# One adaLN step of the second layer amid the first layer's routing, ahead of the first experts' loads

## Chip, cores, metric

One core of one Trainium2 chip. The metric is device microseconds of one execution; of the profiled execution, the span and the granted clock of TensorE are shown beside it. TensorE (PE) multiplies, VectorE (DVE), ScalarE (ACT) and GpSimd (POOL) work on its operands and results, and SyncE (SP) issues nearly all loads and stores; GpSimd issues the indirect ones.

## What is computed

An attention block and then two layers on a main sequence of 512 tokens and a context of 256 tokens, 1024 wide, in float32. Each layer has a mixer (a convolution and a state space scan, with a layer norm and an RMS norm behind them and an output projection) and a mixture of experts: a gate over 4 groups of 4 experts, the two best experts of a token, each with a gate, an up and a down matrix. Both are modulated by adaLN vectors, which come from a condition vector `c` alone:

```
mod = silu(c) @ w_ada[l] + b_ada[l]      # 6 x 1024 per layer and sequence: shift, scale, gate; twice
h   = rmsnorm(x) * (1 + scale) + shift
x   = x + gate * f(h)                    # f: mixer, then experts
```

So layer 1's vectors depend on nothing that layer 0 computes, and may be worked out at any time before layer 1's modulation wants them.

## The kernel before

The kernel is written in Tile: the program gives the operations, a scheduler sets the order of each engine, and buffers come from pools in turn, so that a load waits until the last reader of its slot is done. Matrix products are done as three matmuls of a high and a low part: a weight comes by DMA as a tile of 512 KB (128 x 1024), ScalarE copies it into the high part (L260) and VectorE, or for some tiles GpSimd, subtracts that from it for the low part (L261). The pair is called a split below.

**adaLN.** `ada(l)` (L370) is a generator that makes layer l's vectors in three units u. A unit runs over k = 0 to 7; each k loads two tiles `raw` of `w_ada` (L256, through SP, pool `raw` with four slots) and does four matmuls (L387) into a PSUM tile `ad`. It yields after every second k, which is one step: four loads and eight matmuls. The last step of a unit also copies the sums (L392, ScalarE), turns them (L395) and adds the bias (L397, L405, VectorE). `fill(n)` (L410) advances the generators by n steps, `need(l, c)` until unit c is done. A layer has 12 steps. Where they are called is a table: `FILL[l]` and the strings `SF[l]`. Before, layer 1's steps 1 to 4 stand at the end of layer 0's mixer (`FILL[0][2]` = 4), 5 to 8 in layer 1's scan (`SF[1]` = '02209', L1020), and 9 to 12 behind that scan (the '9' at L885 runs the generator out), beside the convolution, its layer norm (mean L307 and L317, rstd L326 to L360, gelu and gain L897 to L903) and the norm of y (L910).

**Experts.** Layer 0 has six token tiles. At the end of the mixer the output projection (L276) writes `hT` and the context (loads `sg`, stores `cd`). The routing follows: logits (L1257, L1260), their norm (L326 to L335, L1264), bias (L1267), `tokens_out`, which turns the tokens (L1279), scales them (L1282 on VectorE, L1285 on ScalarE with L1286 on GpSimd) and writes them to `t_d` in DRAM (L1287), then the choice of group and experts (L1307 to L1326), lists of tokens (one-hots L1358, matmuls L1390, numbers L1366 to L1377) and the order of the later experts by load (L1598 to L1606, then L1612 and L1613 reorder the choices). An expert e then gathers its tokens (L1434, GpSimd), turns them (L1444), and does its hidden layer (L1474) and its output (L1516); results are scattered by GpSimd (L1535). The first three experts are fixed; later ones are taken by number from `eido` (L1606).

**Loads ahead.** The weights of the first experts are loaded before their turn. `AHEAD[0]` names them by place: a code c is expert c // 3 and its quarter c % 3 (0 and 1 gate and up, 2 down). At place 8 the string '2345' stands for e0's down, e1's two quarters and e1's down, eight loads. They take buffers as `RWS[0]` says, first four `raw`, then alternately `rawm` (four slots of the layer's own pool) and `raw`. `raw` is the pool that the adaLN loads use too.

**Places in the routing.** A small table of functions, `at`, is called at numbered places: position 0 right after the logits, then 1, 2 behind the choice of the experts, 3, 4 and 5 further on. `TPOS` says which function has which position; before, its third is 6, a position at which nothing is called, and `FILL[0][3]` is 0.

Of the kernel before, what the change touches and what calls it, by code (L numbers as in the profile page):

```python
# [34 lines left out]
XW = 1  # L35
HG = 2
HP = 0
FILL = ((1, 0, 4, 0), (0, 0, 0, 0))
SF = ('000111111', '02209')
SCP = (0, 0)  # L40
PB = (3, 3)
# [3 lines left out]
AHEAD = (('', '', '0', '1', '', '', '', '', '2345'), ('', '', '0', '1', '', '', '', '', '2345'))  # L45
TOKV = (0,)
RWS = ("wwwwwwww", "mmmmwwww")
TPOS = (0, 1, 6)

# [152 lines left out]
class Prog:  # L204
# [524 lines left out]
    def mixer(self, l):  # L729
# [4 lines left out]
        with E:  # L734
# [37 lines left out]
            full = [s for s in strs if s.full]  # L772
            self.fill(FILL[l][0])

# [138 lines left out]
            self.need(l, 12)  # L913
            self.fill(FILL[l][2])
            return full
# [149 lines left out]
    def moe(self, l, full):  # L1065
# [22 lines left out]
        with E:  # L1088
# [64 lines left out]
            def gate_up_half(e, q):  # L1153
                if isinstance(e, int) and (e, q) in early:
                    return early[e, q]
                return load_split(wgu_of(e, q), nc.gpsimd if q >= 2 - PL[l] else None)
# [19 lines left out]
            def down_half(e):  # L1176
                if isinstance(e, int) and (e, 2) in early:
                    return early[e, 2]
                return load_split(wd_of(e))

            def ahead(n):
                for c in AHEAD[l][n]:
                    e, q = divmod(int(c, 36), 3)
                    early[e, q] = down_half(e) if q == 2 else gate_up_half(e, q)
# [111 lines left out]
                    nc.scalar.activation(tt[:, 512 * hf:512 * hf + 512], pt, AF.Copy)  # L1296
                nc.sync.dma_start(dst, tt)

            at = dict(zip(TPOS, (tokens_out, lambda: ahead(8), lambda: self.fill(FILL[l][3]))))
            at.get(0, int)()  # L1300
            at.get(1, int)()
            self.mark(f"moe{l}-r")
# [550 lines left out]
```

## Time and profile before

| | |
|---|---|
| median of 3 runs | 1604.54 us (1602.48, 1604.54, 1607.76) |
| the profiled execution | 1599.32 us, span 1597.5 us |
| granted clock of TensorE, mean | 0.938 |
| TensorE busy | 1391.5 us (87%) |
| VectorE busy | 1014.9 us (64%) |
| ScalarE busy | 680.3 us (43%) |
| GpSimd busy | 230.9 us (14%) |
| moved by DMA | 260.79 MB, 163 GB/s in the mean |

Busy time counts instructions that work on data. The idle time before an instruction is given in brackets with what ended it, the releaser. Matmuls are pipelined, so a busy TensorE is not one at its peak. The layer 0 of the text lies between 300 and 1018 us of the span, its routing at 760 to 790; the end of layer 1's scan and norm lies at 1264 to 1305.

### The profile page before, as it was taken

The page shows a single profiled execution, that of the slowest core. Times are in us where ns is not written, and L with a number is a line of the kernel's source. Part 1 is how long each engine was busy: PE and PEld are TensorE (multiplying, and loading weights), DVE is VectorE, ACT ScalarE, POOL GpSimd, SP SyncE. Part 2 cuts the span into 40 slices and gives each one's busy share as a digit, 9 for nine tenths or more (in the row PEclk, how much of TensorE's full clock was granted, in tenths as well). Part 3 has the DMA queues.
Part 4 walks back from the last instruction along what each step waited for, and adds up shares of the span by engine and source line. Part 5 has one row for each costly group of instructions (what it writes and reads, how often), then busy time and mean ns, then how long its engine had stood idle before and what let it go on. Part 6 is the DMA issues. An engine that isn't in the chain of part 4 may idle for free. (4 is left out here: it accounts for less than half of the span.)

```text
span 1597.5 us, 20964 instructions
## 1 busy us (share of the span) xinstructions
PE 1391.5 (87%) x7422; PEld 975.8 (61%) x7422; DVE 1014.9 (64%) x2253; ACT 680.3 (43%) x1237; POOL 230.9 (14%) x205
## 2 busy tenths in 40 slices
PE   7899999979999998899578988589999989678964
PEld 6878766748888743467455566347885446454432
DVE  5877555548999765632783457368995464755445
ACT  5354455324542264433343456244433454424342
POOL 1111100000000221000442334000002200312113
PEclk9999999979999999899789999779999999799977
DMA  6111235221114067532559988602252763579974
GB/s 219 54 54 56 65 130 178 80 79 53 58 62 145 14 211 248 179 112 84 200 175 316 343 269 268 176 33 67 67 184 106 229 235 131 185 279 348 375 285 177
DMA packets 76476, 260.79 MB, mean 163 GB/s; under 512 B 9528, under 2 KB 11960, under 8 KB 76240
## 3 DMA queue, kind: packets, MB, share of 16 engines
q1 hardware_dynamic: 67872, 234.15, 41.8%
q0 software_dynamic: 8496, 25.28, 5.5%
q8 instruction: 59, 0.97, 0.2%
q14 instruction: 49, 0.40, 0.1%
HBM read 231.50 MB, written 33.55 MB: 166 GB/s over the span
## 5 line engine op out<-in xcount | busy, mean ns | idle before, releaser
L276 PE MATMUL mm<-act,uhi 128*128 128x512 f32 (+1 forms) x1504 | 323.3, 361 | 14.6 <-ACT uhi L260 7.7
L276 PEld LDWEIGHTS mm<-act,uhi 128*128 128x128 f32 x1504 | 248.3, 193 | 80.0 <-issue 13.3
L276 PE MATMUL mm<-act,ulo 128*128 128x512 f32 (+1 forms) x752 | 167.9, 357 | 0.6 <-DVE ulo L261 0.6
L276 PEld LDWEIGHTS mm<-act,ulo 128*128 128x128 f32 x752 | 124.9, 192 | 26.2 <-issue 5.1
L814 DVE SCALAR_TENSOR_TENSOR cvx<-vx,pr,cvx 128x456 f32<-128x456 f32 (+18 forms) x176 | 107.9, 616 | 2.3 <-ACT cvx L797 1.2
L260 ACT ACTIVATE uhi<-raw 128x1024 fp32r<-128x1024 f32 x58 | 61.2, 1058 | 109.2 <-PE mm L276 84.4
L387 PE MATMUL ad<-raw,sc 128*32 128x512 f32 x384 | 88.3, 649 | 12.5 <-DMA raw<-wada 12.0
L276 PE MATMUL mm<-whi,act 128*128 128x256 f32 x576 | 84.4, 292 | 10.2 <-ACT whi L260 10.0
L261 DVE TENSOR_TENSOR ulo<-raw,uhi 128x1024 fp32r<-128x1024 f32 x58 | 70.8, 1222 | 25.8 <-ACT uhi L260 9.2
L276 PEld LDWEIGHTS mm<-whi,act 128*128 128x128 f32 x576 | 76.1, 196 | 13.7 <-ACT whi L260 10.0
L1474 PE MATMUL mm<-part,uhi 128*128 128x512 f32 x168 | 55.0, 443 | 18.4 <-ACT part L260 11.8
L276 PE MATMUL mm<-act,whi 128*128 128x512 f32 x256 | 68.9, 411 | 0.2 <-ACT whi L260 0.2
L1474 PE MATMUL mm<-act,uhi 128*128 128x512 f32 x200 | 57.3, 405 | 0.2 <-ACT k L1524 0.2
L814 DVE SCALAR_TENSOR_TENSOR cvc<-vc,pr,cvc 128x241 f32<-128x241 f32 (+14 forms) x120 | 56.7, 472 | 0.5
L276 PEld LDWEIGHTS mm<-act,whi 128*128 128x128 f32 x256 | 47.2, 188 | 14.0 <-issue 3.5
L261 DVE TENSOR_TENSOR act<-rawm,act 128x1024 fp32r<-128x1024 f32 x30 | 39.9, 1331 | 24.3 <-ACT act L260 22.4
L1474 PEld LDWEIGHTS mm<-part,uhi 128*128 128x128 f32 x168 | 32.6, 209 | 32.1 <-ACT part L260 14.8
L1524 ACT ACTIVATE k<-mm 128x512 f32<-128x512 f32 x42 | 24.9, 595 | 60.4 <-PE mm L1516 41.2
L999 POOL TENSOR_TENSOR xw<-xstc,swgtc 128x512 f32<-128x512 f32 x8 | 9.7, 1232 | 278.3 <-ACT xstc L852 174.5
L1535 POOL DMA_INDIRECT acc<-k,idx x19 | 34.4, 1811 | 101.7 <-ACT k L1524 24.3
L261 DVE TENSOR_TENSOR wlo<-raw,whi 128x1024 fp32r<-128x1024 f32 x34 | 41.1, 1220 | 11.5 <-ACT whi L260 11.5
L261 DVE TENSOR_TENSOR act<-raw,act 128x1024 fp32r<-128x1024 f32 x32 | 38.9, 1222 | 14.7 <-ACT act L260 12.3
(528 smaller groups left out, 2828.4 us busy)
## 6 DMA issues: line engine op xcount, KB each, us to landing
raw<-wada SPq DMA_DIRECT2D x96, 512.0 KB, 5.0
raw<-wgu SPq DMA_DIRECT2D x42, 512.0 KB, 6.6
raw<-win SPq DMA_DIRECT2D x40, 512.0 KB, 3.5
rawm<-wgu SPq DMA_DIRECT2D x38, 512.0 KB, 6.8
raw<-wd SPq DMA_DIRECT2D x34, 512.0 KB, 6.4
act<-wgu SPq DMA_DIRECT2D x32, 512.0 KB, 8.5
rawm<-wd SPq DMA_DIRECT2D x30, 512.0 KB, 7.2
raw<-w SPq DMA_DIRECT2D x26, 512.0 KB, 4.6
```

The costliest lines, as they stand in the source:

```text
L260: self.nc.scalar.activation(hi, raw, AF.Copy)
L261: (eng or self.nc.vector).tensor_sub(lo, raw, hi.bitcast(F32))
L276: nc.tensor.matmul(out, lhsT=(ah, ah, al)[p], rhs=(bh, bl, bh)[p], start=(start and p == 0 and i == 0), stop=(stop and p == 2 and i == n - 1))
L387: nc.tensor.matmul(ps[32 * g:32 * g + 32], lhsT=self.sc[:, k, :], rhs=w[g // 2][:, 512 * (g % 2):512 * (g % 2) + 512], start=(k == 0), sto ...
L814: nc.vector.scalar_tensor_tensor(o_, v_, cw[:, l, i, k:k + 1], o_, op0=OP.mult, op1=OP.add)
L999: nc.gpsimd.tensor_tensor(hv(xw), hv(s.xst[:, c]), s.wgt[:, c, 8 * d:8 * d + 8, None].to_broadcast([128, 8, 64]), op=OP.mult)
L1474: nc.tensor.matmul(pg, lhsT=(xh, xl, xh)[p][:, 4 * q + k, :], rhs=(wh, wh, wl)[p][k // 2][:, 512 * (k % 2):512 * (k % 2) + 512], start=(n ...
L1524: nc.scalar.activation(y[:, o], py, AF.Copy)
L1535: nc.gpsimd.indirect_dma_start(out=acc[:, :], out_offset=bass.IndirectOffsetOnAxis(ap=j.sid[:, n:n + 1], axis=0), in_=y, in_offset=None, b ...
```

## The change

One step is put into layer 0's experts, between `tokens_out` and the loads ahead of place 8. Nothing is added: since the generator is taken one step further there, layer 1's scan gets steps 6 to 9 in place of 5 to 8, and three steps stand behind it in place of four. In layer 1 the same place calls `fill(0)`.

```diff
--- before.py
+++ after.py
@@ -35,7 +35,7 @@
 XW = 1
 HG = 2
 HP = 0
-FILL = ((1, 0, 4, 0), (0, 0, 0, 0))
+FILL = ((1, 0, 4, 1), (0, 0, 0, 0))
 SF = ('000111111', '02209')
 SCP = (0, 0)
 PB = (3, 3)
@@ -45,7 +45,7 @@
 AHEAD = (('', '', '0', '1', '', '', '', '', '2345'), ('', '', '0', '1', '', '', '', '', '2345'))
 TOKV = (0,)
 RWS = ("wwwwwwww", "mmmmwwww")
-TPOS = (0, 1, 6)
+TPOS = (0, 1)
 
 
 
@@ -1296,7 +1296,7 @@
                     nc.scalar.activation(tt[:, 512 * hf:512 * hf + 512], pt, AF.Copy)
                 nc.sync.dma_start(dst, tt)
 
-            at = dict(zip(TPOS, (tokens_out, lambda: ahead(8), lambda: self.fill(FILL[l][3]))))
+            at = {TPOS[0]: tokens_out, TPOS[1]: lambda: (self.fill(FILL[l][3]), ahead(8))}
             at.get(0, int)()
             at.get(1, int)()
             self.mark(f"moe{l}-r")
```

The order of instructions moves with it. On SP, at the end of layer 0's output projection, four slots of `raw` (the pool goes round) change hands; `wd` and `wgu` are down and gate/up weights, `wada` adaLN's. Before:

```order
L1137 DMA raw_6939<-wd 128x1024
L1237 DMA cd_6184<-sg_6477 128x256
L1234 DMA sg_6631<-cT 128x256
L1137 DMA raw_6945<-wd 128x1024
L1237 DMA cd_6184<-sg_6564 128x256
L1234 DMA sg_6706<-cT 128x256
L1137 DMA raw_6951<-wgu 128x1024
L1237 DMA cd_6184<-sg_6631 128x256
L1234 DMA sg_6773<-cT 128x256
L1137 DMA raw_6957<-wgu 128x1024
L1237 DMA cd_6184<-sg_6706 128x256
```

Now, from the third of the four adaLN loads on:

```order
L256 DMA raw_6948<-wada 128x1024
L1237 DMA cd_6184<-sg_6631 128x256
L1234 DMA sg_6773<-cT 128x256
L256 DMA raw_6950<-wada 128x1024
L1237 DMA cd_6184<-sg_6706 128x256
L1237 DMA cd_6184<-sg_6773 128x256
L1137 DMA raw_6956<-wd 128x1024
L1137 DMA raw_6962<-wd 128x1024
L1287 DMA t_d_6167<-k_1193_6849 128x1024
```

The four wada loads stand where e0's down and e1's first quarter stood; e0's down comes behind the context's last stores, and e1's six loads and four of e2's come behind the six writes t_d, of which the last row shows the first.

On TensorE, at the logits (L1260) and the token transposes (L1279), before:

```order
L1279 MATMUL mm_6886<-cs,rawm_6181 128x128
L1260 MATMUL ax_6819<-cs,t_1188_6820 128x33 x2
L1279 MATMUL ax_6850<-cs,k_1089_6174 128x128 x4
L1260 MATMUL ax_6819<-cs,t_1189_6824 128x33 x4
L1279 MATMUL ax_6865<-cs,k_1089_6174 128x128 x4
L1279 MATMUL ax_6880<-cs,rawm_6178 128x128 x2
```

Now:

```order
L387 MATMUL ad_6939<-raw_6940,sc 32x512
L1260 MATMUL ax_6819<-cs,t_1188_6820 128x33 x2
L1260 MATMUL ax_6819<-cs,t_1189_6824 128x33 x4
L1279 MATMUL ax_6850<-cs,k_1089_6174 128x128 x4
L1279 MATMUL ax_6865<-cs,k_1089_6174 128x128 x4
L387 MATMUL ad_6939<-raw_6940,sc 32x512
L387 MATMUL ad_6939<-raw_6942,sc 32x512 x2
L387 MATMUL ad_6939<-raw_6948,sc 32x512 x2
L387 MATMUL ad_6939<-raw_6950,sc 32x512 x2
L1279 MATMUL ax_6880<-cs,rawm_6178 128x128 x2
```

One L387 stands ahead of the logits, seven among the transposes.

On VectorE, at the start of the choice (L1307) behind the token writes (L1282), before:

```order
L1282 SCALAR_TENSOR_TENSOR k_1193_6849<-ax_6850,rt_6818,k_1092_6177 128x512
L1267 TENSOR_TENSOR mlg_6817<-mlg_6817,lb_6173 128x40
L1267 TENSOR_TENSOR mlg_6817<-mlg_6817,lb_6173 128x80
L1282 SCALAR_TENSOR_TENSOR k_1196_6864<-ax_6865,rt_6818,k_1092_6177 128x512
L1282 SCALAR_TENSOR_TENSOR k_1199_6879<-ax_6880,rt_6818,row_6183 128x512
L1282 SCALAR_TENSOR_TENSOR k_1202_6894<-ax_6895,rt_6818,row_6183 128x512
L1282 SCALAR_TENSOR_TENSOR k_1205_6909<-ax_6910,rt_6818,row_6183 128x512
L1307 TENSOR_REDUCE mgmx_6989<-mlg_6817 128x6
L1308 TENSOR_TENSOR mgoh_6990<-mlg_6817,mgmx_6989 128x24
L1409 TENSOR_TENSOR mge_6991<-mlg_6817,mgmx_6989 128x24
```

Now, with e0's down, whose splits stood in the output projection before (L261, `act<-raw`):

```order
L1282 SCALAR_TENSOR_TENSOR k_1196_6864<-ax_6865,rt_6818,k_1092_6177 128x512
L1282 SCALAR_TENSOR_TENSOR k_1199_6879<-ax_6880,rt_6818,row_6183 128x512
L1282 SCALAR_TENSOR_TENSOR k_1202_6894<-ax_6895,rt_6818,row_6183 128x512
L1282 SCALAR_TENSOR_TENSOR k_1205_6909<-ax_6910,rt_6818,row_6183 128x512
L261 TENSOR_TENSOR act_6959<-raw_6956,act_6958 128x1024
L261 TENSOR_TENSOR act_6965<-raw_6962,act_6964 128x1024
L1282 SCALAR_TENSOR_TENSOR k_1208_6924<-ax_6925,rt_6818,row_6183 128x512
L1307 TENSOR_REDUCE mgmx_7006<-mlg_6817 128x6
```

Two splits came in ahead of the last L1282 and L1307. Further on, on VectorE still, at the expert order (L1606) and the reordered choices (L1613), before:

```order
L1606 CAST eido_7131<-neidf_7127 128x13
L261 TENSOR_TENSOR ulo_7153<-ax_7161,uhi_7152 128x512
L1613 TENSOR_REDUCE mok_7168<-k_1313_7169 128x78
L1613 TENSOR_REDUCE mow_7177<-k_1315_7178 128x78
L261 TENSOR_TENSOR part_6978<-rawm_6975,part_6977 128x1024
L261 TENSOR_TENSOR part_6984<-raw_6981,part_6983 128x1024
L1423 CAST rc_6171<-mow_7177 128x6x13
L1377 CAST idx_1252_7031<-idf_7200 128x2
```

Now:

```order
L261 TENSOR_TENSOR ulo_7226<-ax_7227,uhi_7225 128x512
L261 TENSOR_TENSOR part_6995<-rawm_6992,part_6994 128x1024
L261 TENSOR_TENSOR part_7001<-raw_6998,part_7000 128x1024
L1606 CAST eido_7148<-neidf_7144 128x13
L1613 TENSOR_REDUCE mok_7185<-k_1318_7186 128x78
L1613 TENSOR_REDUCE mow_7194<-k_1320_7195 128x78
L1377 CAST idx_1257_7048<-idf_7217 128x2
```

The splits of e1's down (`part<-rawm`, `part<-raw`) changed places with L1606 and both L1613.

## Rows read from the trace of the kernel before

**Rows 1.** The page, part 1: busy time of the engines.

```profile
PE 1391.5 (87%) x7422; PEld 975.8 (61%) x7422; DVE 1014.9 (64%) x2253; ACT 680.3 (43%) x1237; POOL 230.9 (14%) x205
```

**Rows 2.** The page, a costly group (out<-in, count | busy, mean ns | idle before) and DMA issues.

```profile
L387 PE MATMUL ad<-raw,sc 128*32 128x512 f32 x384 | 88.3, 649 | 12.5 <-DMA raw<-wada 12.0
...
raw<-wd SPq DMA_DIRECT2D x34, 512.0 KB, 6.4
```

**Rows 3.** Busy us by stretch: PE, PEld, DVE, ACT, POOL; PEclk, DMA share, GB/s.

```profile
740.00:760.00 20.00, 20.00 (x102) 14.15 (x101) 7.19 (x8) 7.38 (x12) 0.00 (x0) 1.00 0.36 115
760.00:780.00 20.00, 8.86 (x64) 6.15 (x62) 14.25 (x43) 7.12 (x13) 7.45 (x6) 0.92 0.51 189
780.00:790.00 10.00, 2.96 (x46) 2.49 (x47) 9.10 (x29) 2.00 (x2) 4.50 (x3) 0.50 0.79 285
830.00:860.00 30.00, 28.84 (x156) 19.73 (x154) 15.42 (x48) 10.33 (x19) 11.87 (x8) 1.00 0.94 310
```

**Rows 4.** Timeline, TensorE, first experts: start, us, what, [idle before <-releaser].

```profile
789.23 1.97 PE L1444 MATMUL ax<-cs,k 128*128 128x128 f32 x8 [2.37 <-DMA k<-t_d,idx]
...
804.20 0.29 PE L1390 MATMUL op<-rc,oh 128*128 128x6 bf16 x6
...
808.00 1.94 PE L1444 MATMUL ax<-cs,k 128*128 128x128 f32 x8 [3.17 <-DMA k<-t_d,idx]
...
816.18 1.27 PE L1444 MATMUL ax<-cs,k 128*128 128x128 f32 x8 [2.29 <-DVE ulo L261]
819.33 1.22 PE L1516 MATMUL mm<-act,hl 128*128 128x512 f32 x2 [1.88 <-DVE hl L261]
...
823.46 1.62 PE L1474 MATMUL mm<-part,uhi 128*128 128x512 f32 x4
```

**Rows 5.** Timeline, SP's own queue, layer 1's adaLN loads.

```profile
1225.84 57.73 SPq L256 DMA_DIRECT2D raw<-wada  x28
```

**Rows 6.** Chain of waits, layer 1's conv and norm: start, us, what.

```profile
1267.86 4.55 DMA raw<-wada
...
1283.24 4.62 DMA raw<-wada
```

**Rows 7.** Timeline, TensorE, layer 0's routing.

```profile
767.80 0.63 PE L1279 MATMUL ax<-cs,rawm 128*128 128x128 f32 x4 [2.41 <-DVE mlg L1264]
```

**Rows 8.** Timeline, VectorE, layer 0's routing and first experts.

```profile
773.28 0.16 DVE L1307 TENSOR_REDUCE mgmx<-mlg 128x6 f32<-128x24 f32 x1
...
774.40 1.22 DVE L1309 TENSOR_TENSOR mgoh<-mgoh,cs 128x24 f32<-128x24 f32 x1
...
777.70 0.26 DVE L1309 TENSOR_TENSOR moh<-moh,cs 128x96 f32<-128x96 f32 x1
...
797.34 1.21 DVE L1613 TENSOR_REDUCE mow<-k 128x78 f32<-128x1014 f32 x1 [1.55 <-POOL k L1612]
798.46 1.22 DVE L261 TENSOR_TENSOR part<-rawm,part 128x1024 fp32r<-128x1024 f32 x1
```

**Rows 9.** Timeline, GpSimd, the same stretch.

```profile
770.59 4.99 POOL L1286 TENSOR_TENSOR k<-k,row 128x512 f32<-128x512 f32 x4
784.77 1.16 POOL L1434 DMA_INDIRECT k<-t_d,idx  x1 [9.19 <-DMA rawm<-wgu]
...
801.80 1.00 POOL L1434 DMA_INDIRECT k<-t_d,idx  x1 [4.50 <-DVE mow L1425]
807.26 1.20 POOL L1434 DMA_INDIRECT k<-t_d,idx  x1 [4.46 <-issue]
811.87 2.38 POOL L261 TENSOR_TENSOR act<-raw,act 128x1024 fp32r<-128x1024 f32 x1 [3.41 <-ACT act L260]
```

**Rows 10.** Timeline, SP's own queue, layer 0's token writes.

```profile
769.43 7.23 SPq L1287 DMA_DIRECT2D t_d<-k  x6
```

**Rows 11.** Timeline, ScalarE, layer 1's norm of y.

```profile
1290.02 0.62 ACT L304 ACTIVATE t2x<-yx 128x512 f32<-128x512 f32 x1
```

**Rows 12.** Timeline, VectorE, layer 1's norm of y.

```profile
1293.80 1.23 DVE L261 TENSOR_TENSOR ulo<-raw,uhi 128x1024 fp32r<-128x1024 f32 x1
```

## Prediction

> **What bounds the kernel now.** I read the page first: TensorE is the busiest engine, 1391.5 us, 87% of the span [rows 1], and the adaLN matmuls L387 cost it 88.3 us in 24 steps, 3.7 us a step, with 12.5 us of idle time before them, nearly all for the loads raw<-wada [rows 2]. Whether a moved step gains anything is decided by the two places that it leaves and enters, so I read those next, in the busy time by stretch and the timelines.
>
> The place it enters, layer 0's routing, is not bound by TensorE: from 760 to 780 us it works 8.86 us of 20, from 780 to 790 only 2.96 at a granted clock of 0.50 (the lower level, 1.2 GHz, after it had stood idle for most of ten us), while VectorE works 14.25 and 9.10 [rows 3]. It is a chain of small VectorE instructions that ends in the first gather. Ahead of it, 740 to 760, TensorE is full (20.00 of 20), and the chip's DMA engines work at 0.36 [rows 3]. Behind it come the first experts: TensorE stands 2.37, 3.17, 2.29 and 1.88 us for the first gather, the third, and two splits [rows 4], until the second half of the experts starts at 823.46; from 830 to 860 the DMA share is 0.94 and TensorE 28.84 of 30 [rows 3].
>
> The place it leaves is the end of layer 1's conv and norm. Of the 28 loads raw<-wada there, issued in 57.73 us, each takes 2.06 us [rows 5], and the chain of waits runs twice through them, 4.55 and 4.62 us [rows 6].
>
> **The change, part by part.** No step is added: 12 in layer 1's vectors before and after. One step is 4 loads of 512 KB, 8 matmuls (384 / 24 = 16 records) and no unit's end, so no L392, L395 or L397.
>
> *Layer 0, out-projection.* Four slots of `raw` that carried weights of e0's down and e1's first quarter now carry wada, so four splits leave ScalarE and VectorE. TensorE is full in that stretch [rows 3], so I take 0 here; at best 1 us.
>
> *Routing.* One L387 stands ahead of L1260: 3.7/8 = 0.5 us, 0.9 taken for that it delays both rows of logits. The other seven, 3.2 us, stand between the L1279 transposes. Before, TensorE idled 2.41 us there [rows 7]; so they push the later transposes by 0.9 + 3.2 - 2.4 = 1.7 us, and with them the token writes L1282. The two down splits of e0, 1.22 each (by the one at 798.46 [rows 8]), now stand on VectorE just ahead of the last L1282 and L1307 (third fence pair of the change). Their loads can issue only when the seven L387 have freed `raw`, near 769, and took 6.4 us to land at the page's median [rows 2], near 774 to 775; L1307 was at 773.28 [rows 8]. Then 2.4 us of splits follow: L1307 near 775 to 777, so +1.8 to +4. Against that, the first L1309, which took 1.22 us beside GpSimd's token adds where the next took 0.26 without them [rows 8], would come after the adds end at 775.58 [rows 9], which gives back 1.0. I take **+1.8** for the start of the experts, bounds 0.5 and 4.
>
> Here a rule is weighed. L1309 took 0.96 us longer beside GpSimd's adds, 1.25 us each, than alone [rows 8, 9]. The Trainium skill, SBUF — State Buffer, section "SBUF: two separate sides", says that a VectorE instruction with two SBUF inputs and a GpSimd instruction that reads SBUF share a port pair as a lock: whoever comes second stands still for the whole instruction. The rows agree. By it a split that falls among the adds would take 1.22 + 1.25 instead of 1.22, twice: +2.5 on the chain, a rival below; the sum leaves it out, since by the times above the splits fall at the adds' end.
>
> *SP and the loads.* e1's six loads now stand behind the six token writes t_d (first fence pair), so after 776.7 (769.43 + 7.23 [rows 10]); before, four of them and two of e2 were in SBUF by then. Ten loads go out there. The DMA share was 0.79 from 780 to 790 [rows 3], so the first gather, 784.77 to the tokens at 789.23 [rows 9, 4], shares with more: 0 to 1.7 us later (its later brother took 6.2, 801.80 to 808.00 [rows 9, 4]). I take 0 beyond the 1.8, for e1's weights are not wanted before 798.
>
> *Experts.* On VectorE the splits of e1's down now stand ahead of L1606 and both L1613 (last fence pair). Before, the second reduction ran from 797.34 to 798.55 and the splits came after it, from 798.46 on [rows 8]; now splits first, tied to ScalarE's split behind e0's first matmuls (+1.8), then 2 x 1.21: near 802.6. The third gather, 801.80 before, goes near 804.2, and its tokens stand at 810.4 (+2.4). e1's hidden layer has run by then in one piece. But the list L1390 for the next gather, at 804.20 before, now comes behind those tokens: 810.4 + 1.94 for the tokens and half a us of other work, 813; its gather, 3.1 us later as before (807.26), at 816; with 6.2 to land, tokens at 822.3 in place of 816.18; and L1516, which stands behind them, at 823.5 in place of 819.33 [rows 9, 4]. **+4.2** for the second half of the experts. Beyond 830 DMA and TensorE are both nearly full, so I let it pass to the layer's end whole. Bounds: +0.5 (TensorE's 3.17 + 2.29 + 1.88 = 7.3 us of idle time there swallow the rest) and +6.6 (a GpSimd split of 2.38 ahead of that gather, a rival).
>
> *Layer 1's tail.* Three steps instead of four. Four loads fewer are 8.2 us of queue, 3.7 us of TensorE. But between the two wada waits stands a chain that needs no wada: the layer norm's L326, L356, L360 and L902, then ScalarE's activations and splits in its order, up to L304 at 1290.02, for which the norm of y waits [rows 11]. It moves by the L387 taken out between L307 and L317, two pairs, 1.1 us. And VectorE now has both ulo splits, 1.22 us each, inside the y norm's rsqrt chain where one stood at 1293.80 [rows 12]: -1.1 + 1.2 = **0**; bounds -4 (half of the queue's 8.2) and +1.5.
>
> **Sum**: 0 + 4.2 + 0 = +4, on the profiled execution 1599.32 + 4 = 1603.3. That execution is 5.2 below the median of the runs shown, 1604.54; against it the forecast is 1608.5. A measurement of this kernel tells 0.3%, 4.8 us, from no change, so +4 counts as the same.
>
> **Rivals.**
> - *The tail comes free.* If the chain in layer 1 followed the loads, the queue's 8.2 us would go and the experts' 7.3 us of stalls layer 0's part: -8.2, 1596.3; with a part of it held by ScalarE, -6, 1598.5. For it: 4.55 and 4.62 us of the chain are wada [rows 6]. Against: ScalarE's queue at 1290.02. It decides if L304 of y starts over 3 us earlier.
> - *The fourth gather sticks behind GpSimd.* The split moved ahead of it (2.38 us [rows 9]) waits for ScalarE's half, whose load is now the tenth in SP's queue. From the point where that half is later than 816, the gather is at 818.4 or more, and the first gather pays its 1.7 too: 4.2 + 2.4 + 1.7 = +8.3, 1612.8. Slower.
> - *The port lock* on both down splits: 4.2 + 2.5 = +6.7, 1611.2. Slower.
> - *Hidden anyway.* The 1.8 us of the routing vanish in the experts' stalls and the tail gives nothing: 1604.5. For it: TensorE's 7.3 us of stalls between 808 and 823 [rows 4]. That the step would not move at all is excluded by the order of instructions.
>
> **How the numbers follow.** Forecast (+0.5 to +8, centre +4) 0.42, of which 0.28 within 0.3% and 0.14 above; tail free 0.24 (0.22 faster, 0.02 same); gather 0.17 and lock 0.05, slower; hidden 0.12, same. So faster 0.22, same 0.42, slower 0.36. The range goes from between these two prices of the free tail, 1597, to the gather's +8.3 with 2.2 for the routing's upper bound (4 for 1.8), 1615.
>
> **What would show it.** Right: four raw<-wada issued between 705 and 740; L1307 at 775 to 777; third gather near 804, tokens of the fourth near 822, e2's hidden 3 to 6 us later than 823.46 by the same origin; layer 1's y norm to out-projection unchanged within 1.5 us. Wrong: an L1307 no later than before, tokens of the fourth gather no later than 818, or a wait on raw<-wada gone from layer 1's chain with the out-projection 3 us or more earlier against the layer's start.

## Result and the profile after

| | before | changed |
|---|---|---|
| median | 1604.54 us (5 runs, 1600.15 to 1607.76) | 1618.46 us (5 runs, 1608.38 to 1619.34) |
| ratio to before | | 1.0105, 95% interval 1.0072 to 1.0138 |
| the profiled execution | 1599.32 us, span 1597.5 us | 1618.46 us, span 1616.7 us |
| granted clock, mean | 0.938 | 0.928 |

The change made the kernel slower by 1.05% by the ratio, some 17 us, and its median is above the 1615 that the range reached to. The two medians lie 13.9 us apart; all kernels below are compared by the ratio, whose intervals reach 0.2 to 0.3% to either side. The page of the changed kernel has TensorE 9 us busier for the same number of instructions, at a lower mean granted clock; VectorE and GpSimd are 2 us busier each, ScalarE is as before:

```profile
PE 1400.1 (87%) x7422; PEld 985.1 (61%) x7422; DVE 1017.2 (63%) x2253; ACT 680.8 (42%) x1237; POOL 233.1 (14%) x205
```

So no work was added; something waits. To see where, I count from the start of the first logits matmul L1260 (763.11 us before, 760.98 now, within what the kernels below, early5 apart, differ by at that point, 758 to 764). From there to layer 1's first residual (L1801) it takes 266.7 us before and 282.8 now, **+16.1**; from that to the last normalised y (L910) 272.9 and 276.6, **+3.7**; the rest of the span 294.8 and 296.3, +1.5. With the -2.1 of the start these make the 19.2 us between the two spans.

The busy time by stretch, as in [rows 3]: the stretch and its length, PE, PEld, DVE, ACT, POOL (instructions), granted clock, DMA share, GB/s.

```profile
740.00:760.00 20.00, 20.00 (x97) 12.87 (x95) 1.99 (x3) 4.39 (x10) 0.00 (x0) 1.00 0.04 14
760.00:780.00 20.00, 8.73 (x65) 5.74 (x64) 16.63 (x44) 7.96 (x12) 8.14 (x6) 0.87 0.63 231
780.00:790.00 10.00, 1.89 (x36) 1.48 (x36) 9.53 (x32) 3.17 (x3) 2.70 (x2) 0.50 1.02 392
830.00:860.00 30.00, 28.27 (x152) 22.19 (x151) 17.74 (x41) 13.62 (x23) 11.19 (x7) 0.95 0.66 194
```

From 740 to 760, where TensorE is full, the DMA share fell from 0.36 to 0.04: the adaLN loads were there by then, and SP's next loads wait for their slots. They go out at once later: 780 to 790 has 1.02 where 0.79 stood. And from 830 to 860 0.66 stands in place of 0.94.

TensorE's timeline behind the routing, as in [rows 4]:

```profile
790.55 1.97 PE L1444 MATMUL ax<-cs,k 128*128 128x128 f32 x8 [2.88 <-DMA k<-t_d,idx]
...
795.32 1.12 PE L1444 MATMUL ax<-cs,k 128*128 128x128 f32 x4 [1.60 <-DMA k<-t_d,idx]
...
814.15 1.94 PE L1444 MATMUL ax<-cs,k 128*128 128x128 f32 x8 [5.52 <-DMA k<-t_d,idx]
...
826.82 0.44 PE L1444 MATMUL ax<-cs,k 128*128 128x128 f32 x1 [7.53 <-DMA k<-t_d,idx]
826.92 1.20 PE L1516 MATMUL mm<-act,hl 128*128 128x512 f32 x2
...
832.44 1.37 PE L1474 MATMUL mm<-part,uhi 128*128 128x512 f32 x4
```

Counted from L1260, the first tokens stand at 29.6 us (26.1 before), the third at 53.2 (44.9), the fourth at 65.8 (53.1), after a wait of 7.53 us for their gather; e0's output (`hl`) right behind them at 65.9 (56.2), and e2's hidden layer at 71.5 (60.4). So the tokens' delay grows from gather to gather, +3.5, +8.3 and +12.7 us, and e2's hidden layer is 11.1 us late. VectorE's timeline, as in [rows 8], shows a large part of the reason:

```profile
770.87 4.33 DVE L261 TENSOR_TENSOR act<-raw,act 128x1024 fp32r<-128x1024 f32 x2
...
775.78 0.16 DVE L1307 TENSOR_REDUCE mgmx<-mlg 128x6 f32<-128x24 f32 x1
...
801.26 1.52 DVE L261 TENSOR_TENSOR part<-raw,part 128x1024 fp32r<-128x1024 f32 x1
802.69 0.47 DVE L1606 CAST eido<-neidf 128x13 int32<-128x13 f32 x1
...
804.19 1.19 DVE L1613 TENSOR_REDUCE mow<-k 128x78 f32<-128x1014 f32 x1
...
817.03 1.22 DVE L261 TENSOR_TENSOR act<-rawm,act 128x1024 fp32r<-128x1024 f32 x1
818.16 2.33 DVE L1377 CAST idx<-idf 128x2 int32<-128x2 f32 x1
```

The two splits of e0's down in the routing took 4.33 us in place of 2.44; e1's down splits end at 802.78, and only then come L1606 and both L1613, to 805.38 (798.55 before). A split stands ahead of the fourth list's numbers (817.03), and their conversion L1377 took 2.33 us, where the one of the third list, at 805.31, took 0.15. GpSimd, as in [rows 9]:

```profile
768.17 3.74 POOL L1286 TENSOR_TENSOR k<-k,row 128x512 f32<-128x512 f32 x3
772.17 1.95 POOL L1286 TENSOR_TENSOR k<-k,row 128x512 f32<-128x512 f32 x1 [0.26 <-ACT k L1285]
...
785.01 1.16 POOL L1434 DMA_INDIRECT k<-t_d,idx  x1 [10.89 <-DMA raw<-wgu]
...
806.22 1.00 POOL L1434 DMA_INDIRECT k<-t_d,idx  x1 [2.63 <-DVE ulo L261]
818.02 2.44 POOL L261 TENSOR_TENSOR act<-raw,act 128x1024 fp32r<-128x1024 f32 x1 [10.81 <-ACT act L260]
820.76 0.96 POOL L1434 DMA_INDIRECT k<-t_d,idx  x1 [0.30 <-DVE wsl L1396]
```

GpSimd's adds ran beside the first pair of slow VectorE instructions (768.17 on), its split at 818.02 beside the slow L1377, and the fourth gather stands behind that split, at 820.76, 59.8 us from L1260 (44.1 before). SP's queue shows what is late behind it. The loads of a pair of later experts (`act<-wgu`, L1145, eight issues) go out in all kernels here some five us after e2's hidden layer has begun; the first of them, before:

```profile
829.52 13.70 SPq L1145 DMA_DIRECT2D act<-wgu  x8
```

and in the changed kernel, where the row above it is one of the experts' own loads ahead, now behind the token writes:

```profile
776.34 1.22 SPq L1137 DMA_DIRECT2D raw<-wgu  x2
...
837.27 15.42 SPq L1145 DMA_DIRECT2D act<-wgu  x8
```

The pair's loads are 7.75 us later, 9.9 counted from L1260, and take 1.7 us longer to issue.

### The profile page after: what moved, and what is told of

Its sections match the earlier page's. It is cut to its first block, busy times and chain, and to the rows that moved or that the text cites. A ratio compares the mean times of both kernels' runs of the same rounds, so it can differ in the third digit from the quotient of the medians.

```text
span 1616.7 us, 20964 instructions
## 1 busy us (share of the span) xinstructions
PE 1400.1 (87%) x7422; PEld 985.1 (61%) x7422; DVE 1017.2 (63%) x2253; ACT 680.8 (42%) x1237; POOL 233.1 (14%) x205
## 5 line engine op out<-in xcount | busy, mean ns | idle before, releaser
L260 ACT ACTIVATE uhi<-raw 128x1024 fp32r<-128x1024 f32 x58 | 61.1, 1058 | 108.7 <-PE mm L276 81.3
L387 PE MATMUL ad<-raw,sc 128*32 128x512 f32 x384 | 89.6, 661 | 5.0 <-DMA raw<-wada 4.5
L261 DVE TENSOR_TENSOR ulo<-raw,uhi 128x1024 fp32r<-128x1024 f32 x58 | 70.8, 1222 | 25.7 <-ACT uhi L260 9.4
L1474 PE MATMUL mm<-part,uhi 128*128 128x512 f32 x168 | 56.3, 451 | 20.0 <-ACT part L260 12.8
L261 DVE TENSOR_TENSOR act<-rawm,act 128x1024 fp32r<-128x1024 f32 x30 | 42.1, 1404 | 26.6 <-ACT act L260 24.5
L1474 PE MATMUL mm<-act,uhi 128*128 128x512 f32 x200 | 56.4, 403 | 1.4 <-ACT k L1524 1.4
L1444 PE MATMUL ax<-cs,k 128*128 128x128 f32 x232 | 35.6, 301 | 20.6 <-DMA k<-t_d,idx 20.6
L1474 PEld LDWEIGHTS mm<-part,uhi 128*128 128x128 f32 x168 | 33.5, 214 | 32.8 <-ACT part L260 14.2
L261 DVE TENSOR_TENSOR part<-rawm,part 128x1024 fp32r<-128x1024 f32 x26 | 31.6, 1223 | 29.4 <-ACT part L260 21.2
L1235 DVE SCALAR_TENSOR_TENSOR hT<-mm,mod,hT 128x512 f32<-128x512 f32 x16 | 12.0, 751 | 60.0 <-PE mm L276 60.0
```

What stands on the lines that cost most here:

```text
L260: self.nc.scalar.activation(hi, raw, AF.Copy)
L261: (eng or self.nc.vector).tensor_sub(lo, raw, hi.bitcast(F32))
L387: nc.tensor.matmul(ps[32 * g:32 * g + 32], lhsT=self.sc[:, k, :], rhs=w[g // 2][:, 512 * (g % 2):512 * (g % 2) + 512], start=(k == 0), sto ...
L1444: nc.tensor.transpose(pt[:, 128 * k:128 * k + 128], j.xg[:, 512 * hf + 128 * k:512 * hf + 128 * k + 128], self.ident)
L1474: nc.tensor.matmul(pg, lhsT=(xh, xl, xh)[p][:, 4 * q + k, :], rhs=(wh, wh, wl)[p][k // 2][:, 512 * (k % 2):512 * (k % 2) + 512], start=(n ...
```

## The experiments

The theory after this reading (A): what costs is that e0's and e1's loads changed places with the step's, and that the splits, which go where their loads are, stand ahead of the lists that the third and fourth gather need; layer 1 gives nothing back. The rivals: the routing costs over 20 and layer 1 gives some back (B); the step's own work costs wherever it stands in the routing (C), or its matmuls delay the routing (E).

**early5.** The step elsewhere, ahead of the output projection.

```diff
-FILL = ((1, 0, 4, 1), (0, 0, 0, 0))
+FILL = ((1, 0, 5, 0), (0, 0, 0, 0))
```

> The moved step stands at the end of layer 0's mixer with the four others (five there), the routing is left alone, layer 1's tail has one step fewer as in the change. Theory A (the first experts of layer 0 lose because loads and splits changed places; layer 1's tail gives nothing): the step's 3.7 us of TensorE ahead of the projection and no gain in layer 1, 0 to +4 us against the kernel before, layer 0's tokens of the fourth list no later than before relative to the logits. Theory B (layer 1's tail gives back 4 to 8 us and the routing costs over 20): -4 to 0 us, and layer 1 from its start to the end of the norm of y is 4 us or more shorter than before.

Measured: 1.0019 of before (0.9995 to 1.0043), +3 us. The logits start 5.2 us later than before (768.28), the fourth tokens at 53.4 from there (53.1 before). Layer 1 from its first residual to the last y took 276.1 us (272.9): no relief. Theory B falls.

**behind.** The step at the same place of the program, behind the loads.

```diff
-            at = {TPOS[0]: tokens_out, TPOS[1]: lambda: (self.fill(FILL[l][3]), ahead(8))}
+            at = {TPOS[0]: tokens_out, TPOS[1]: lambda: (ahead(8), self.fill(FILL[l][3]))}
```

> The same step at the same place in the program, but behind the loads ahead of place 8 in place of ahead of them, so e0's down and e1's first half quarters keep their slots and their early issue. Theory A (displaced loads and the splits behind them): most of the loss goes, 0 to +6 us against before in place of +14. Theory C (the step's own loads and matmuls in the routing, wherever in it): still +10 to +14.

Measured: 0.9972 (0.9944 to 1.0000), 4.5 us faster than before, with an interval that reaches to no change. e2's hidden layer starts 55.3 us from L1260. The same loads and matmuls in the same routing cost nothing once the experts' loads go first: C falls.

**dummy.** A copy of the step in the routing, layer 1 untouched.

```diff
-            at = {TPOS[0]: tokens_out, TPOS[1]: lambda: (self.fill(FILL[l][3]), ahead(8))}
+            def dummy():
+                ps = self.psum("ad", 1)
+                for k in range(2):
+                    w = [self.load(I["wada"][1, 0, k][:, 1024 * i:1024 * i + 1024]) for i in range(2)]
+                    for g in range(4):
+                        o = 512 * (g % 2)
+                        nc.tensor.matmul(ps[32 * g:32 * g + 32, :512], lhsT=self.sc[:, k, :],
+                                         rhs=w[g // 2][:, o:o + 512], start=(k == 0), stop=(k == 1))
+            at = {TPOS[0]: tokens_out, TPOS[1]: lambda: (l == 0 and dummy(), ahead(8))}
```

> The kernel before with an extra copy of one step (four loads, eight matmuls, its sums used by nothing) at the place of the change; layer 1 keeps all its steps, as before. It prices the routing alone. Theory A: layer 0 as in the change, +14 us, and layer 1 as before, so +12 to +17 in all, the same as the change. Theory B: +18 to +25, since the relief of layer 1 is missing.

Measured: 1.0088 (1.0059 to 1.0117), +14 us, the change's loss within the intervals; e2's hidden at 70.9. Layer 0 from L1260 to layer 1's first residual took 281.4 us (282.8 in the change). So the loss is layer 0's, as theory A expected, and the step taken out of layer 1 is worth nothing that shows.

**after_pl and before_pl.** GpSimd's share of the splits in layer 0 given to VectorE, in the changed kernel and in the kernel before.

```diff
-PL = (1, 0)
+PL = (0, 0)
```

> The changed kernel with GpSimd's share of the splits of layer 0's second quarters given to VectorE. Theory A1 (the fourth gather stands behind GpSimd's split and its numbers wait for that split on VectorE): the wait of 7.53 us ahead of the fourth tokens falls to 3 or less and the kernel gains 3 to 6 us on the change. Theory A2 (the late list, behind the third tokens, is what counts): the wait falls by 2 to 3 us only and the time stays within 3 us of the change, or is worse by VectorE's extra work.

> The kernel before with GpSimd's splits of layer 0 given to VectorE, the control for the same edit to the change, which brought that back to the time before. If the edit repairs what the change spoils (the fourth gather behind GpSimd's split), this one is within 4 us of the kernel before. If GpSimd's splits are a loss in the later experts of either kernel, this one is 8 us or more faster.

Measured: the changed kernel so edited 1.0006 (0.9980 to 1.0032), 16 us less than the change; the kernel before 0.9944 (0.9920 to 0.9968), 9 us faster. So the first looked like a repair, and the control shows that half of it is a gain of its own: against before_pl the change still costs 1.0006 / 0.9944 = 1.0062, 10 us. The fourth tokens' wait of 7.53 us is gone (0.63, for TensorE's own work), but they stand at 63.3 from L1260, since the third are later, at 57.7. A1 was right on the wait; its gain of 3 to 6 us was too small. The control came out as the second reading of its expectation had it, 8 us or more faster. Of that gain one place is found: between 820 and 1000 us TensorE's largest wait for a GpSimd split (L1474 for `part`, 4.3 us, once) is gone in before_pl. The rest of the 9 us isn't accounted for.

**after_pl2.** One split alone, e2's second quarter, from GpSimd to VectorE.

```diff
-                return load_split(wgu_of(e, q), nc.gpsimd if q >= 2 - PL[l] else None)
+                return load_split(wgu_of(e, q), nc.gpsimd if q >= 2 - PL[l] and not (isinstance(e, int) and e == 2) else None)
```

> The changed kernel with one split alone, that of e2's second quarter, given from GpSimd to VectorE: the one that the change put ahead of the fourth gather. If that split is what makes the loss, the wait of 7.53 us ahead of the fourth tokens falls to 4 or less and the kernel is 4 to 8 us faster than the change, +6 to +10 against before. If the late list behind the third tokens makes it, the wait stays over 5 and the kernel within 3 us of the change.

Measured: 1.0049 (1.0031 to 1.0067), 9 us less than the change, for one instruction. On TensorE the fourth tokens still wait, 5.27 us, now for VectorE's split `act<-raw`, which took the place of GpSimd's:

```profile
820.17 2.07 PE L1516 MATMUL mm<-act,hh 128*128 128x512 f32 x4 [0.39 <-ACT hh L260]
...
827.68 1.94 PE L1444 MATMUL ax<-cs,k 128*128 128x128 f32 x8 [5.27 <-DVE act L261]
```

The order is that of the change: four matmuls of e0's output (`hh`, from 820.17), the fourth tokens, then the rest. So the wait came as the second reading had it and the time as the first (+8 us against before, of +6 to +10). The fourth gather goes out at 58.3 us from L1260, only 1.5 earlier than in the change, and e2's hidden layer 2.4 earlier (69.1 and 71.5). From L1260 to layer 1's first residual it is 276.8 and 282.8, so 3.6 us more are won behind e2's start; the later stages of the two profiled executions differ by 1 us. That this one split counts for much of the loss is shown; how it does, beyond the 2.4, is not.

**after_a234 and before_a234.** e1's down taken out of the loads ahead, in the changed kernel and before; it is then loaded in e1's turn. On VectorE L1606 and both L1613 stand ahead of its splits again.

```diff
-AHEAD = (('', '', '0', '1', '', '', '', '', '2345'), ('', '', '0', '1', '', '', '', '', '2345'))
+AHEAD = (('', '', '0', '1', '', '', '', '', '234'), ('', '', '0', '1', '', '', '', '', '2345'))
```

> The changed kernel with e1's down taken out of the loads ahead of place 8, so that it is asked for in e1's turn; on VectorE L1606 and both L1613 stand ahead of its two splits again, as before the change, while e0's down splits stay in the routing and the step stays where it is. Theory A (the late expert order and reordered choices, and with them the third and fourth gather): most of the loss goes, 0 to +6 us against the kernel before, and the fourth tokens stand 8 us or more earlier than in the change relative to the logits. Theory A0 (the routing's own delay and the adaLN step's loads): still +11 or more.

> The same edit to the kernel before, a control: by every theory within 4 us of the kernel before. If it is 6 us or more faster, the edit helps by itself and says less about the change.

Measured: 1.0040 (1.0021 to 1.0060), +6.4 us, and 0.9983 (0.9961 to 1.0005) for the control. The third tokens are at 49.4 us from L1260 (53.2 in the change), the fourth at 60.5 (65.8): 5.3 earlier, not 8. The fourth gather stands ahead of GpSimd's split again. This repairs 10 us of 17, and 1.0040 / 0.9983 = 1.0057 is left.

**after_both.** Both edits to the changed kernel (the `AHEAD` line of after_a234 and the `load_split` line of after_pl2).

> The changed kernel with both repairs at once: e1's down asked for in its turn, and e2's second quarter split by VectorE. If the two repair one thing (the third and fourth gather being late), the time is as with either, +5 to +8 us against before. If they repair two things that add, it is back at the time before, -2 to +2.

Measured: 1.0030 (1.0007 to 1.0052), +4.8 us; e2's hidden at 66.8. Together they repair little more than after_a234 alone (1.0040), which is nearer to one thing mended (+5 to +8) than to two (-2 to +2), though the interval, +1.1 to +8.3 us, touches both. With either edit the fourth gather no longer stands behind GpSimd's split, but it is 5.3 us earlier than in the change in after_a234 and 1.5 in after_pl2, so this need not be what they have in common. What makes the 0.3% that is left no run tells.

**dummyload.** The dummy step with matmuls of 32 columns: the loads without TensorE's 3.7 us, layer 1 untouched.

```diff
-                        nc.tensor.matmul(ps[32 * g:32 * g + 32, :512], lhsT=self.sc[:, k, :],
-                                         rhs=w[g // 2][:, o:o + 512], start=(k == 0), stop=(k == 1))
+                        nc.tensor.matmul(ps[32 * g:32 * g + 32, :32], lhsT=self.sc[:, k, :],
+                                         rhs=w[g // 2][:, o:o + 32], start=(k == 0), stop=(k == 1))
```

> The kernel before with four extra adaLN loads at the place of the change and matmuls of 32 columns only, which free the slots; layer 1 as before. GpSimd's split stands behind the fourth gather here, as before the change. Theory A: what is left without the late fourth gather is e0's down splits in the routing and e1's loads behind the token writes, +5 to +8 us. Theory E (the step's matmuls in the routing delay it): 0 to +2.

Measured: 1.0012 (0.9985 to 1.0039), +2 us. The time is theory E's (0 to +2), its mechanism is not: the routing ends as late as in the change (L1329 19.6 us from L1260; 17.5 before, 19.9 in the change). The fourth tokens are as late too (64.9), but on TensorE all of e0's output (`hl` from 61.1) stands ahead of them, where in the change `hl` stands behind; GpSimd's split is behind the fourth gather, which goes out at 53.4 (59.8 in the change); and e2's hidden layer starts at 65.7. So late tokens by themselves cost little here: a wait counts by what is queued behind it. And the loads' displacement by itself, which is the same in this kernel as in dummy, does not make the loss either. Which of the two, the order on TensorE or the one on GpSimd, makes the difference to dummy's 14 us this run doesn't tell.

**warm2.** Theory D, from layer 1's windows below: 12 matmuls, whose sums nobody uses, added to layer 1's tail of the kernel behind.

```diff
                     self.put_split(s.mx, i, v)
+                    if l == 1:
+                        px = self.mm()
+                        for g in range(3):
+                            nc.tensor.matmul(px[32 * g:32 * g + 32], lhsT=self.sc[:, i, :],
+                                             rhs=s.mx[0][i].bitcast(F32), start=True, stop=True)
```

> The kernel with the step behind the loads (0.28% faster than before), with 12 added matmuls in layer 1's tail whose sums nobody uses, fed by the layer norm's results, so that TensorE has work where the taken step left it idle. Theory D (in the tail TensorE falls to the lower clock for want of work, and that eats the relief): the granted clock between 255 and 270 us after layer 1's first residual goes from 0.50 to near 1.00, the sums L307 and L347 for the norm of y from 1.9 to 1.1 us, and the norm of y ends 1 to 3 us earlier than in that kernel, the median 1 to 3 us below it. If ScalarE's order alone holds the tail, the clock rises and the time stays within 1 us or gets worse.

Measured: 0.9975 (0.9955 to 0.9994) of before, where the kernel behind has 0.9972: no difference that can be told, so the time is as the rival reading had it. Inside the profile the clock rose as said, L307 and L347 took 1.05 us each (1.75 and 1.86 in behind), and the stage took 271.5 us to the last y where behind took 273.6. The stretches, columns as above:

```profile
1277.50:1282.50 5.00, 4.79 (x32) 1.40 (x32) 2.95 (x6) 4.38 (x9) 0.00 (x0) 1.00 0.63 221
1282.50:1287.50 5.00, 4.84 (x27) 4.06 (x25) 3.47 (x11) 2.08 (x3) 0.00 (x0) 1.00 0.23 66
```

against the kernel behind at the same distance from layer 1's first residual (255 to 260 and 260 to 265 us):

```profile
1278.70:1283.70 5.00, 1.91 (x10) 1.11 (x10) 2.61 (x6) 4.62 (x9) 0.00 (x0) 0.94 0.68 259
1283.70:1288.70 5.00, 4.31 (x14) 3.12 (x13) 1.75 (x8) 2.49 (x3) 0.00 (x0) 0.50 0.00 0
```

That the added matmuls brought the clock back is shown. The 2.1 us of the stage agree with it in one execution each, but lie within what the kernels differ by there (272 to 277), and the end of the program does not show them.

**behind_pl_a234.** The three edits whose ratio was below 1 by themselves, together; of the three, only before_pl's interval lies clear of 1.

> The step behind the loads, GpSimd's splits of layer 0 given to VectorE, e1's down asked for in its turn: each was faster than before by itself (0.28%, 0.56%, 0.17%). If they add: 1.0% faster than before, 1585 us by a median of 1600. If they gain from the same waits: 0.5 to 0.6%.

Measured: 0.9946 (0.9929 to 0.9963), 7.1 us faster in the median (1594.31). So they do not add; that they gain from the same waits is the reading of the expectation, and no run shows which. It and before_pl (0.9944) are the fastest kernels of the study, faster than both that were compared.

What goes with the order of the kernels is the start of e2's hidden layer (its first L1474, on `part`), counted from the first L1260, both from TensorE's timeline, in us:

| kernel | e2's hidden | first `act<-wgu` | ratio |
|---|---|---|---|
| behind | 55.3 | 61.0 | 0.9972 |
| before_a234 | 55.5 | 60.9 | 0.9983 |
| warm2 | 55.5 | 61.1 | 0.9975 |
| before | 60.4 | 66.4 | 1 |
| early5 | 60.7 | 66.8 | 1.0019 |
| dummyload | 65.7 | 70.6 | 1.0012 |
| after_both | 66.8 | 73.2 | 1.0030 |
| after_a234 | 67.6 | 73.6 | 1.0040 |
| after_pl2 | 69.1 | 74.7 | 1.0049 |
| dummy | 70.9 | 75.5 | 1.0088 |
| the change | 71.5 | 76.3 | 1.0105 |
| behind_pl_a234 | 55.7 | 61.3 | 0.9946 |
| before_pl | 57.4 | 63.0 | 0.9944 |
| after_pl | 69.2 | 74.9 | 1.0006 |

The last three have no GpSimd splits in layer 0 and are to be compared with each other. The pair's loads start 4.6 to 6.4 us after e2's hidden layer in all of them. The ratios follow this order but for neighbours whose intervals overlap (dummyload and early5 among them). It is an order, not a price: after_pl and after_pl2 start e2 at the same 69 us and differ by 0.4%. With the same loads ahead of the experts' a kernel takes 1.0012 (dummyload) to 1.0105 (the change) of the time before, as the engines' orders come out.

## Why the prediction was wrong

The direction of the sum, +4, was right, and so was the chain that it follows (late lists, late gathers, L1516 behind them); its size was not. The step that failed is the experts' term, +4.2: it moved the first experts by the routing's 1.8 us only and put the first gathers' own delay at 0, and it let the sum reach the layer's end unchanged. Measured were +11.1 us at e2's hidden layer and +16.1 at the layer's end.

- *Out-projection, 0.* Right as far as it can be told: the logits start within the scatter of the kernels.
- *Routing, +1.8.* Nearly right at its end: the first matmul behind the choice (L1329) is 19.9 us from L1260 (17.5), +2.4. Its parts were not, and they made up for each other by luck. L1307 at 775.78 lies inside the 775 to 777 named, but only because the logits began 2.1 us earlier; from L1260 it is 4.6 us later. The loads of e0's down were issued at 764.41 and split from 768.41 on, four us, not 6.4, so the splits fell among GpSimd's adds and not at their end, and took 4.33 us; the L1308 and L1309 behind them then took 0.18 each (0.88 and 1.22 before).
- *The port lock*, left out of the sum with a chance of 0.05, shows twice in the rows above: 4.33 - 2.44 = 1.9 us on the down splits and 2.33 - 0.15 = 2.2 on L1377. The rule of the Trainium skill, SBUF — State Buffer, section "SBUF: two separate sides", agrees with both: each slow VectorE instruction has a GpSimd instruction beside it in the rows above. L1377 has one input, in SBUF, so of the section's two kinds it would be the one in a two-port mode, which no run here shows. Such waits were not new. Before, an instruction of the expert order and one of a later list had them, L1600 and L1374, beside GpSimd's splits of 787.22 and 811.87 [rows 9] (0.33 and 0.16 us in the changed kernel):

```profile
786.74 3.05 DVE L1600 TENSOR_TENSOR lt<-nu 128x169 bf16<-128x169 f32 x1
...
811.98 2.29 DVE L1374 TENSOR_TENSOR idf<-idf 128x1 f32<-128x1 f32 x1
```

VectorE's busy time grew by 2.3 us in all. So the change mostly moved such waits, onto instructions that the experts stood behind.

- *First gathers, 0 beyond the routing.* Both came later. The first was issued 2.4 us later from L1260, with the routing, and its tokens were 3.5 late. The second was issued 2.4 us later too, and its tokens were 5.4 late, after a wait of 1.60 us on TensorE (795.32 above; 792.04 before, without a wait). The DMA engines' share was 1.02 from 780 to 790 (0.79 before), with the experts' loads going out there.
- *Third gather, +2.4.* Measured 45.2 - 38.7 = +6.5. I moved ScalarE's split of e1's down by the routing's 1.8 only; it waits for TensorE's first matmuls of e0 (the releaser below), which waited for both gathers, and so it came 6.1 us later from L1260. Before and now:

```profile
795.04 1.06 ACT L260 ACTIVATE part<-rawm 128x1024 fp32r<-128x1024 f32 x1 [0.31 <-PE mm L1474]
```

```profile
798.98 1.06 ACT L260 ACTIVATE part<-rawm 128x1024 fp32r<-128x1024 f32 x1 [0.21 <-PE mm L1474]
```

VectorE's two splits, L1606 and both L1613 then ran one behind the other, as the forecast had them.

- *Fourth gather and L1516, +4.2.* The forecast had the gather +8.7 us, at 816; it was +15.6. L1516 was +9.7 (65.9 to 56.2), and e2's hidden layer +11.1. The list came behind the third tokens as said, and the rival came true on top: ScalarE's half of the split of e2's second quarter was done at 817.94, past the 816 named, and the gather stood behind GpSimd's 2.44 us. Of the 6.9 us beyond the forecast, 4.1 came with the third gather, 1.7 with its landing (7.9 us, not 6.2), and by estimate 1.4 with GpSimd's split, less 0.4 that the list came sooner behind the tokens: the gather is 4.5 us behind the list's L1390 at 816.31 where the forecast had 3.1, and in after_pl2 it is 1.5 earlier. The two rivals' prices on top of the forecast's own, 4.2 + 2.4 + 1.7 + 2.5 = 10.8, come near the 11.1, but by luck, since the parts measured are others. I gave the rivals chances as alternatives, though they could come together, and did.
- *Beyond 830 the delay passes on whole.* It grew: +11.1 at e2's hidden, +16.1 at the layer's end. In after_a234, after_pl2 and after_both +7.3, +8.7 and +6.5 became +10.1, +10.1 and +9.5. But early5, level with before at e2's hidden layer (+0.3), is +3.3 at the layer's end as well, and dummyload's +5.4 became +3.2. So part of the growth may belong to the one profiled execution of the kernel before that all are measured against. Where the last 1 to 5 us are lost was not tried and stays open.
- *Layer 1's tail, 0.* Right in what it gives: the changed kernel's own +3.7 lies beyond the +1.5 named, but eight kernels with a step fewer took 272.0 to 276.7 us there and five with all steps 272.2 to 276.9, so no relief and no loss can be told. Both ulo splits stood inside the rsqrt chain as said (1311.20 and 1312.42). The reason was incomplete; see the clock below.

Of the signs named beforehand, four wada loads went out from 701.88 to 734.88 (705 to 740 was named). The third gather was to be near 804 and was at 806.22, the fourth tokens near 822 and were at 826.82, both 2.1 us later still when counted from the logits. e2's hidden layer was to be 3 to 6 us later and was 11.1.

## What to carry to other kernels

A load that enters a rotating pool ahead of others does not only take its own time: it pushes every later load of the pool back, the splits follow their loads, and what a scheduler then puts behind them in an engine's order (here a list, a gather, an expert's output) can cost several times the moved work: 17 us for a step of 3.7. It need not: with narrower matmuls the same displaced loads came out at 2 us. Put the filler behind the loads that have a due time: the same step there took 0.9972 of the time before. And ask of rivals whether they can come true together; if they can, their chances are not those of alternatives.

## What was not expected of the hardware

The taken step left TensorE with less to do in layer 1's tail, and its clock fell. The kernel before, from 1280 to 1300 us; columns as above:

```profile
1280.00:1290.00 10.00, 6.48 (x31) 1.45 (x32) 5.61 (x10) 7.03 (x11) 0.00 (x0) 1.00 0.87 299
1290.00:1295.00 5.00, 5.00 (x27) 3.55 (x27) 3.55 (x8) 3.13 (x5) 0.00 (x0) 1.00 0.74 246
1295.00:1300.00 5.00, 4.35 (x17) 2.84 (x16) 3.37 (x15) 0.30 (x1) 0.00 (x0) 1.00 0.85 261
```

The changed kernel at the same stage, some 13 to 18 us later:

```profile
1290.00:1295.00 5.00, 2.75 (x14) 1.61 (x14) 2.69 (x14) 1.15 (x3) 0.00 (x0) 0.87 0.83 274
1295.00:1300.00 5.00, 5.00 (x19) 0.94 (x18) 2.72 (x4) 2.63 (x3) 0.00 (x0) 0.50 0.41 134
1300.00:1305.00 5.00, 2.27 (x14) 1.00 (x9) 1.82 (x5) 3.74 (x7) 0.00 (x0) 0.84 0.80 256
1305.00:1310.00 5.00, 3.50 (x10) 1.76 (x10) 1.14 (x2) 3.52 (x6) 0.00 (x0) 0.50 0.06 26
```

The granted clock is 1.00 throughout before, the level of 2.4 GHz, with TensorE at 6.48 of 10 in the emptiest stretch; in the changed kernel it works 2.75 of 5, and the next five us are at 0.50, 1.2 GHz, and so again from 1305 on, after 2.27 of 5. Three groups of matmuls stand in the chain there, L360 for the layer norm, then L307 and L347 for the norm of y. Before:

```profile
1281.10 1.12 PE L360 MATMUL ax<-t2x,cs 128*128 128x512 f32 x2 [1.36 <-DVE t2x L356]
...
1290.69 1.04 PE L307 MATMUL ax<-t2x,cs 128*32 128x512 f32 x2
...
1292.47 1.01 PE L347 MATMUL ax<-cs,t2x 128*128 128x1 f32 x8
```

and now, in the same order:

```profile
1294.43 2.08 PE L360 MATMUL ax<-t2x,cs 128*128 128x512 f32 x2 [2.25 <-DVE t2x L356]
...
1305.82 1.91 PE L307 MATMUL ax<-t2x,cs 128*32 128x512 f32 x2 [2.85 <-ACT t2x L304]
1308.42 1.86 PE L347 MATMUL ax<-cs,t2x 128*128 128x1 f32 x8 [0.69 <-ACT t2x L310]
```

1.12, 1.04 and 1.01 us became 2.08, 1.91 and 1.86. All eight kernels with a step fewer and no filler show a stretch of five us at 0.50 to 0.53 there. Of those with all steps dummy, before_pl and before_a234 show 1.00 as before does, dummyload, whose step has 32 columns in place of 512 in the routing, 0.82 to 0.84 (0.66 where the five us are laid 2.5 us later). warm2, a step fewer but with the filler, has 1.00 back. So work that fills an engine's gaps beside a chain of short matmuls is not free to take away: here it held the clock for them. What that costs the stage is not shown: after_pl, with a stretch at 0.53, took 272.0 us for it, and before_a234, at 1.00 throughout, 273.9.
